# Value stage of an expert-retrieval block: a fixed order for VectorE's work on the operands of a key

## The chip, the cores and the metric

One core of one Trainium2 chip runs the whole program, a single launch. The metric is device time in microseconds of that core. Engines: PE is TensorE (matrix products, with weight loads listed apart as PEld), DVE is VectorE, ACT is ScalarE, POOL is GpSimd, SP is SyncE; SPq is the queue of transfers that SP issues. In this kernel SP issues nearly all plain loads and POOL the gathers.

## What is computed

Two layers of a diffusion backbone on 640 tokens (512 latent, 128 context), width 1024. Each layer is a mixer of three branches and then a product-key expert retrieval. Only the second half of the retrieval is touched here:

```python
u = jnp.take(u_tab, e, axis=0)
act = jax.nn.gelu(jnp.einsum("cd,chkd->chk", hc, u).astype(jnp.float32))
vv = jnp.take(v_tab, e, axis=0)
return jnp.einsum("chk,chkd->cd", (gate * act).astype(hc.dtype), vv)
```

There are 16384 experts, 128 chosen by each token. The table of values `v_tab` has 16384 rows of 1024 floats in each layer.

## The kernel before

The 640 tokens are five tiles of 128. For the tiles in the dense part the kernel doesn't gather: it multiplies all 16384 rows with the tokens and sets what was not chosen to zero by a gate matrix. The first dense stage (`dense_u`, L1675) makes the activations of three tiles and stores them to DRAM as `ad`. The second (`dense_v`, L1693) is the **value stage**: it runs over 128 keys, and a key is a block of 128 rows of the value table.

For each key `operands` (L1705) makes what the products need:

- `vr`, the 128 rows of the table (512 KB, loaded at L1708 through SP, three buffers).
- `gt`, the gates of four keys at once (1024 KB, L1713 through SP, two buffers). Four keys that share one `gt` are called a **group** below.
- `gl`, the gated activations, three buffers. ACT copies one tile's part from `gt` (L1719); SP loads the other three tiles' activations into the rest (192 KB, L1721), and DVE multiplies them with the gates (L1722: *gating*).
- `ash` and `asl`, the high and low half of `gl`: ACT casts (L1725), DVE subtracts (L1726). Three buffers each.
- `us`, the high and low halves of the two 512-column halves of `vr`, made by the helper `split` (L415 on ACT, L416 on DVE). Four buffers of each kind, so two keys' worth.

`products` (L1730) then issues 24 matmuls of 128x512 for a key: four token tiles, two column halves, and for each of these high by high, high by low and low by high (L1737). They add up in eight PSUM banks over all keys.

Beside this, the weave of L1636 puts the *sparse passes* of the remaining tile or tiles into the program: POOL gathers one row for each of 128 tokens (L1529, 512 KB, four buffers) and DVE multiplies or adds it (L1793 `pscr`, L1809 `acc`).

Dependences hold a value back until its buffer is free: `gl` of key n+3 may be written only when L1726 of key n has read the old one, `vr` of key n+3 when both L416 of key n are done, `us` of key n+2 when the products of key n are done. `gt` of a group may be loaded when the last gating and copy of the group two before it are done.

The order of instructions on each engine is not that of the code: a scheduler makes it when the program is built, from its own estimates. Each engine then takes its instructions strictly in that order. `keep_in_program_order` pins only the sparse passes among themselves.

Of the kernel before, what the change touches and what calls it, by code (L numbers as in the profile page):

```python
# [20 lines left out]
D = 1024  # L21
# [25 lines left out]
USB = 4  # L47
# [201 lines left out]
NOSYNC = mybir.DependencyInfo(mybir.DependencyClass.NoSync, mybir.DependencyReason.DATA)  # L249
# [11 lines left out]
class K:  # L261
# [1431 lines left out]
    def dense_v(self, l, gr, ar, grow, x, xr, pool, kp, nxt, sps):  # L1693

        nc, I = self.nc, self.I
        v = nc.vector
        ns, S = NT - ND, ND - NU
        acc = {}  # L1700
        vt = I["pev"]
        gts = {}
        dp = pool

        def operands(n, lo, hi, pool):  # L1705
            w, CT = 128 * (hi - lo), 128 // GC
            vr = dp.tile([128, D], F32, tag="raw", name=self.nm("vr"), bufs=RAWB)
            nc.sync.dma_start(vr, bass.AP(tensor=vt.tensor, offset=vt.offset + (16384 * l + n) * D, ap=[[128 * D, 128], [1, D]]))  # L1708
            if (n // GN, lo, hi) not in gts:
                gts.clear()  # L1710
                t = dp.tile([128, ND * CT, GN, GC], F32, tag="gt", name=self.nm("gt"))
                n0 = n // GN * GN
                nc.sync.dma_start(t[:, CT * lo:CT * hi], gr[CT * lo:CT * hi, :, n0:n0 + GN, :].rearrange("c p n t -> p c n t"))  # L1713
                gts[n // GN, lo, hi] = t
            g = gts[n // GN, lo, hi][:, :, n % GN, :]
            gl = dp.tile([128, 128 * ND], F32, tag="gl", name=self.nm("gl"), bufs=3)
            g3 = gl.rearrange("p (c t) -> p c t", t=GC)
            if lo < S:
                nc.scalar.copy(g3[:, CT * lo:CT * S], g[:, CT * lo:CT * S])  # L1719
            if hi > S:  # L1720
                nc.sync.dma_start(gl[:, 128 * S:], ar[n])  # L1721
                v.tensor_tensor(g3[:, CT * S:], g3[:, CT * S:], g[:, CT * S:], op=ALU.mult)  # L1722
            a = slice(128 * lo, 128 * hi)
            ah, al = (pool.tile([128, 128 * ND], F32R, tag=t, name=self.nm(t), bufs=3 if pool is dp else None) for t in ("ash", "asl"))
            nc.scalar.copy(ah[:, a], gl[:, a])  # L1725
            v.tensor_tensor(al[:, a], gl[:, a], ah[:, a].bitcast(F32), op=ALU.subtract)  # L1726
            vs = [self.split(pool, vr[:, o:o + 512], [128, 512], "us", USB if pool is dp else None) for o in range(0, D, 512)]
            return ah, al, vs

        def products(n, i, hf, ops):  # L1730
            ah, al, vs = ops
            vh, vl = vs[hf]
            if i not in acc:
                acc[i] = [self.psum(t) for t in ACCT[i]]
            c = slice(128 * i, 128 * i + 128)
            for q, (a, b) in enumerate(((ah, vh), (ah, vl), (al, vh))):
                nc.tensor.matmul(acc[i][hf], a[:, c], b, start=n == first(i) and q == 0, stop=n == 127 and q == 2)  # L1737

        def key(n, lo, hi):
            ops = operands(n, lo, hi, dp)  # L1740
            for hf in range(2):
                for i in range(lo, hi):
                    products(n, i, hf, ops)

        m = 0

        def first(i):
            return 0 if i >= S else m

        def done(i):  # L1750
            for hf in range(2):
                d = slice(512 * hf, 512 * hf + 512)
                t = pool.tile([128, 512], F32, tag="gl", name=self.nm("dr"), bufs=3)
                v.tensor_tensor(t, acc[i][hf], grow[1 if ns + i < 4 else 0][:, d], op=ALU.mult)
                self.x_add(ns + i, 512 * hf, t)

        while not self.gated or m % GN:
            key(m, S, ND)
            m += 1
            yield 1.3 * NU  # L1760
        follow = self.x_open(l, x, xr, kp, nxt)
        step = max(1, (128 - m) // max(m, 1))
        late = iter(range(m))
        for n in range(m, 128 - GE):
            key(n, 0, ND)
            yield 1.3 * ND
            if (n - m) % (GN * step) == GN * step - 1 or n == 127 - GN:
                for j in islice(late, None if n == 127 - GN else GN):
                    key(j, 0, S)
                    yield 1.3 * S  # L1770
        zp = xr.enter_context(self.pool("pz", "right", GE - 1))
        tail = [(n, operands(n, 0, ND, zp if n < 127 else dp)) for n in range(128 - GE, 128)]
        run(sps)
        for i in range(ND + 2):
            if i < ND:
                for n, ops in tail:
                    for hf in range(2):
                        products(n, i, hf, ops)
            if i > 0:
                next(follow)  # L1780
            if i < ND:
                done(i)
        self.hT = ret(follow)
# [66 lines left out]
def run(g):  # L1850
    for _ in g:
        pass


def ret(g):
    while True:
        try:
            next(g)
        except StopIteration as e:
            return e.value  # L1860
# [47 lines left out]
```

## Time and profile before

| | us |
|---|---|
| median of 3 runs | 6227.96 |
| lowest and highest of them | 6202.13, 6228.57 |
| the profiled execution's own time | 6218.67 |
| its span, first to last instruction | 6216.6 |

| engine | busy us | share of the span |
|---|---|---|
| PE | 5582.4 | 90% |
| PEld | 4880.7 | 79% |
| DVE | 4162.3 | 67% |
| ACT | 2626.0 | 42% |
| POOL | 1706.5 | 27% |

The mean granted clock of TensorE is 0.934 of full speed. The value stage's products run from 2287 us to 3133 us in layer 0 and from 5390 us to 6201 us in layer 1, a good quarter of the span. Busy shares are means over stages with different limits, so the stage has to be read by itself.

### The profile page before, as it was taken

What the parts mean: (1) busy time and instruction counts of PE and PEld (TensorE: products, weight loads), DVE (VectorE), ACT (ScalarE), POOL (GpSimd) and SP (SyncE); (2) the same over time, 40 slices, a digit from 0 to 9 for tenths busy, and PEclk for the clock granted to TensorE, in tenths of its full rate; (3) what the DMA queues carried; (4) which work ended last, traced back from release to release, by engine and by line L of the source; (5) the groups of instructions that cost most, each with busy time, mean ns of one, the idle gap of its engine ahead of it and who ended that gap; (6) DMA issues with size and microseconds to landing.
All of it is one profiled execution on the core that took longest, in us unless ns stands there. A gap on an engine that the chain in (4) does not pass through costs nothing. (4 is left out here: it accounts for less than half of the span.)

```text
span 6216.6 us, 93203 instructions
## 1 busy us (share of the span) xinstructions
PE 5582.4 (90%) x32966; PEld 4880.7 (79%) x32966; DVE 4162.3 (67%) x9449; ACT 2626.0 (42%) x6243; POOL 1706.5 (27%) x1604
## 2 busy tenths in 40 slices
PE   7899899899799988988988998999987999888988
PEld 5787778789799987767766887788887999777776
DVE  6545545369988876666765545453799888666667
ACT  6244344433366652322352443443333666422223
POOL 1212222101533333333222222231024333233331
PEclk9899899999899999999998888999999999999999
DMA  6212222532589998888852122224325999988886
GB/s 235 73 54 72 69 78 67 181 122 71 156 300 350 341 340 278 296 278 294 270 189 72 48 71 73 76 69 158 103 92 162 340 344 343 325 292 294 283 302 228
DMA packets 630596, 1210.49 MB, mean 195 GB/s; under 512 B 127728, under 2 KB 352368, under 8 KB 630128
## 3 DMA queue, kind: packets, MB, share of 16 engines
q1 hardware_dynamic: 413840, 574.87, 28.1%
q0 software_dynamic: 132768, 469.70, 22.7%
q10 hardware_dynamic: 83520, 159.97, 6.8%
q8 instruction: 259, 4.24, 0.3%
q14 instruction: 209, 1.71, 0.1%
HBM read 1020.28 MB, written 184.05 MB: 194 GB/s over the span
## 5 line engine op out<-in xcount | busy, mean ns | idle before, releaser
L440 PE MATMUL mm<-hT,us 128*128 128x384 f32 x6144 | 1184.4, 348 | 131.4 <-ACT gl L1689 58.6
L440 PEld LDWEIGHTS mm<-hT,us 128*128 128x128 f32 x6144 | 1096.2, 195 | 156.7 <-ACT gl L1689 61.8
L469 PE MATMUL mm<-hT,ws 128*128 128x320 f32 x5472 | 1041.6, 336 | 10.7 <-POOL ws L416 6.7
L1529 POOL DMA_INDIRECT ga<-in_peu,ei x512 | 606.2, 1184 | 1249.9 <-DVE pscr L1793 1139.7
L469 PEld LDWEIGHTS mm<-hT,ws 128*128 128x128 f32 x5472 | 876.0, 202 | 72.3 <-issue 19.6
L1793 DVE SCALAR_TENSOR_TENSOR pscr<-ga,ht 128x1024 bf16<-128x1024 f32 x512 | 627.4, 1225 | 31.5 <-DMA ga<-in_peu,ei 28.8
L416 POOL TENSOR_TENSOR ws<-wr,ws 128x512 fp32r<-128x512 f32 x228 | 302.6, 1329 | 1053.9 <-ACT ws L415 1042.2
L1737 PE MATMUL g<-us,ash 128*128 128x512 f32 x1024 | 349.5, 410 | 192.7 <-DVE us L416 166.5
L1529 POOL DMA_INDIRECT ga<-in_pev,ei x256 | 339.1, 1325 | 630.8 <-DVE acc L1809 570.2
L1719 ACT COPY gl<-gt 128x128 f32<-128x128 f32 x256 | 76.3, 299 | 1010.7 <-DVE asl L1726 984.9
L1722 DVE TENSOR_TENSOR gl<-gl,gt 128x384 f32<-128x384 f32 x256 | 142.2, 556 | 519.5 <-DMA gl<-ad 498.5
L415 ACT CAST ws<-wr 128x512 fp32r<-128x512 f32 x340 | 210.3, 620 | 477.1 <-PE mm L469 186.0
L1737 PEld LDWEIGHTS g<-us,ash 128*128 128x128 f32 x1024 | 199.0, 195 | 268.0 <-DVE us L416 200.2
L416 POOL TENSOR_TENSOR us<-ur,us 128x512 fp32r<-128x512 f32 x132 | 202.6, 1557 | 752.3 <-ACT us L415 566.5
L1659 DVE TENSOR_TENSOR oh<-cst,gm 128x512 f32<-128x512 f32 x512 | 333.2, 684 | 111.4 <-PE g L1663 86.8
L415 ACT CAST us<-ur 128x512 fp32r<-128x512 f32 x512 | 307.1, 616 | 237.8 <-PE mm L440 221.6
L416 DVE TENSOR_TENSOR us<-vr,us 128x512 fp32r<-128x512 f32 x528 | 361.1, 687 | 14.5 <-ACT us L415 14.4
L1662 ACT ACTIVATE oh<-oh,gm 128x128 f32<-128x128 f32 x1024 | 338.3, 394 | 24.2 <-DVE oh L1659 20.3
L415 ACT CAST us<-vr 128x512 fp32r<-128x512 f32 x528 | 324.2, 617 | 32.6 <-PE mm L1737 23.7
L1737 PE MATMUL a<-us,ash 128*128 128x512 f32 x1024 | 331.2, 404 | 4.2 <-ACT ash L1725 4.2
L1737 PE MATMUL c<-us,ash 128*128 128x512 f32 x1024 | 333.1, 406 | 0.0
L1737 PE MATMUL mm<-us,ash 128*128 128x512 f32 x1024 | 327.8, 401 | 0.0
(381 smaller groups left out, 10908.2 us busy)
## 6 DMA issues: line engine op xcount, KB each, us to landing
vr<-in_pev SPq DMA_DIRECT2D x264, 512.0 KB
ur<-in_put SPq DMA_DIRECT2D x256, 512.0 KB
gd<-gmo ACTq DMA_DIRECT2D x128, 512.0 KB
gt<-gd SPq DMA_DIRECT2D x62, 1024.0 KB
wr<-in_win POOLq DMA_DIRECT2D x114, 512.0 KB
aw<-in_adaw SPq DMA_DIRECT2D x96, 512.0 KB
ad<-gl ACTq DMA_DIRECT2D x256, 192.0 KB
gl<-ad SPq DMA_DIRECT2D x256, 192.0 KB
```

What stands on the lines that cost most here:

```text
L415: nc.scalar.copy(h, src)
L416: (eng or nc.vector).tensor_tensor(lo, src, h.bitcast(F32), op=ALU.subtract)
L440: self.nc.tensor.matmul(out, a, b, start=i == 0, stop=i == len(ops) - 1)
L469: self.nc.tensor.matmul(ps, w[k][i], hT[j][:, k, a:b], start=k == i == j == 0, stop=k == 7 and i == 1)
L1529: self.nc.gpsimd.indirect_dma_start(out=t, out_offset=None, in_=self.I[tab], in_offset=bass.IndirectOffsetOnAxis(ap=ei[:, s:s + 1], axis=0))
L1659: v.tensor_tensor(oh[k], iota, T[k][:, t0:t0 + 4, None].to_broadcast([128, 4, 128]), op=ALU.is_equal)
L1662: nc.scalar.mul(oh[0][:, j, :], oh[0][:, j, :], T[2][:, t0 + j:t0 + j + 1])
L1719: nc.scalar.copy(g3[:, CT * lo:CT * S], g[:, CT * lo:CT * S])
L1722: v.tensor_tensor(g3[:, CT * S:], g3[:, CT * S:], g[:, CT * S:], op=ALU.mult)
L1737: nc.tensor.matmul(acc[i][hf], a[:, c], b, start=n == first(i) and q == 0, stop=n == 127 and q == 2)
L1793: pin(v.scalar_tensor_tensor(scr, u, 1.0, h, op0=ALU.mult, op1=ALU.mult, accum_out=dots[:, s:s + 1]))
```

## The change

In `operands` the splits of the two halves of `vr` move from the end to the place right behind the load of `vr`. And all DVE instructions that `operands` makes are chained, each to the one made before it, over all keys, by a dependence that only fixes the order and makes nobody wait on a semaphore. So DVE's order for a key is: low half of the first 512 columns, low half of the second, gating, low half of the activations; then the same for the next key. Sparse passes may still stand anywhere between. No instruction is added or removed, no size or buffer count changes.

```diff
@@ dense_v
         acc = {}
+        self.lastv = None
         vt = I["pev"]
@@ operands
             nc.sync.dma_start(vr, bass.AP(tensor=vt.tensor, offset=vt.offset + (16384 * l + n) * D, ap=[[128 * D, 128], [1, D]]))
+            made = nc.cur_bb.bb.instructions
+            at = len(made)
+            vs = [self.split(pool, vr[:, o:o + 512], [128, 512], "us", USB if pool is dp else None) for o in range(0, D, 512)]
             if (n // GN, lo, hi) not in gts:
...
             v.tensor_tensor(al[:, a], gl[:, a], ah[:, a].bitcast(F32), op=ALU.subtract)
-            vs = [self.split(pool, vr[:, o:o + 512], [128, 512], "us", USB if pool is dp else None) for o in range(0, D, 512)]
+            for i in made[at:]:
+                if i.engine == mybir.EngineType.DVE:
+                    if self.lastv is not None:
+                        self.tc.add_manual_dep(i, self.lastv.name, NOSYNC, reason="hold_order")
+                    self.lastv = i
             return ah, al, vs
```

Line numbers of the changed kernel: L1709 loads `vr`, L1717 `gt`, L1725 `gl`; L1723 is the copy, L1726 the gating, L1729 and L1730 the halves of the activations, L1745 the products, L1801 and L1817 the sparse passes.

What this makes of the order, around key 36 of layer 0 (keys counted from 0 in the order of the program; the number behind a name tells buffers' uses apart). **DVE, before**: `vr_24273` and `us_24286`, `us_24290` belong to key 36, `us_24240` to key 35, `asl_24282` to key 36, `asl_24330` to key 37, `gl_24373` to key 38, `gl_24418` to key 39.

```order
L1722 TENSOR_TENSOR gl_24373<-gl_24373,gt_24275 128x384
L1726 TENSOR_TENSOR asl_24282<-gl_24277,ash_24281 128x512
L416 TENSOR_TENSOR us_24240<-vr_24225,us_24239 128x512
L1793 SCALAR_TENSOR_TENSOR pscr_20803,do_20802<-ga_24267,ht_14562 128x1024
L1793 SCALAR_TENSOR_TENSOR pscr_20803,do_20802<-ga_24270,ht_14562 128x1024
L416 TENSOR_TENSOR us_24286<-vr_24273,us_24285 128x512
L1722 TENSOR_TENSOR gl_24418<-gl_24418,gt_24275 128x384
L1726 TENSOR_TENSOR asl_24330<-gl_24325,ash_24329 128x512
L416 TENSOR_TENSOR us_24290<-vr_24273,us_24289 128x512
```

**DVE, changed**: here `us_24276`, `us_24280`, `gl_24285` and `asl_24290` are all of key 36, and `us_24326` opens key 37.

```order
L1801 SCALAR_TENSOR_TENSOR pscr_20803,do_20802<-ga_24267,ht_14562 128x1024
L416 TENSOR_TENSOR us_24276<-vr_24273,us_24275 128x512
L1801 SCALAR_TENSOR_TENSOR pscr_20803,do_20802<-ga_24270,ht_14562 128x1024
L416 TENSOR_TENSOR us_24280<-vr_24273,us_24279 128x512
L1726 TENSOR_TENSOR gl_24285<-gl_24285,gt_24283 128x384
L1730 TENSOR_TENSOR asl_24290<-gl_24285,ash_24289 128x512
L1801 SCALAR_TENSOR_TENSOR pscr_20803,do_20802<-ga_24317,ht_14562 128x1024
L416 TENSOR_TENSOR us_24326<-vr_24323,us_24325 128x512
```

Before, the gating stood three keys ahead of the splits it stands between; now it stands behind those of its own key. The number of sparse passes for a key (two, two, one) is as it was.

**SP, before** (loads for keys 34 to 39; `vr_24180`, `vr_24225`, `vr_24273` and `vr_24323` are keys 34 to 37, `gl_24277`, `gl_24325`, `gl_24373` and `gl_24418` keys 36 to 39, `gt_24466` the gates of keys 40 to 43):

```order
L1708 DMA vr_24180<-in_pev 128x1024
L1713 DMA gt_24466<-gd_14612 128x16x128
L1708 DMA vr_24225<-in_pev 128x1024
L1721 DMA gl_24277<-ad_14613 128x384
L1721 DMA gl_24325<-ad_14613 128x384
L1708 DMA vr_24273<-in_pev 128x1024
L1721 DMA gl_24373<-ad_14613 128x384
L1708 DMA vr_24323<-in_pev 128x1024
L1721 DMA gl_24418<-ad_14613 128x384
```

**SP, changed** (`vr_24180` to `vr_24323` are keys 34 to 37 again, `gl_24190`, `gl_24235`, `gl_24285` keys 34 to 36, `gt_24283` the gates of keys 36 to 39):

```order
L1709 DMA vr_24180<-in_pev 128x1024
L1717 DMA gt_24283<-gd_14612 128x16x128
L1725 DMA gl_24190<-ad_14613 128x384
L1709 DMA vr_24225<-in_pev 128x1024
L1725 DMA gl_24235<-ad_14613 128x384
L1709 DMA vr_24273<-in_pev 128x1024
L1725 DMA gl_24285<-ad_14613 128x384
L1709 DMA vr_24323<-in_pev 128x1024
```

The activations' load of a key now follows the load of its own rows instead of running two keys ahead, and beside the load of key 34's rows stands the block of keys 36 to 39 where before it was the block of keys 40 to 43.

**ACT, before** (casts at L415 of keys 34 and 35, copies of keys 38 and 39, casts at L1725 of keys 35 and 36):

```order
L415 CAST us_24190<-vr_24180 128x512
L1725 CAST ash_24231<-gl_24227 128x512
L415 CAST us_24194<-vr_24180 128x512
L1719 COPY gl_24373<-gt_24275 128x128
L415 CAST us_24235<-vr_24225 128x512
L1725 CAST ash_24281<-gl_24277 128x512
L415 CAST us_24239<-vr_24225 128x512
L1719 COPY gl_24418<-gt_24275 128x128
```

**ACT, changed** (casts at L415 and at L1729 of keys 34 and 35, copies of keys 36 and 37):

```order
L415 CAST us_24182<-vr_24180 128x512
L1723 COPY gl_24285<-gt_24283 128x128
L415 CAST us_24186<-vr_24180 128x512
L1729 CAST ash_24194<-gl_24190 128x512
L415 CAST us_24227<-vr_24225 128x512
L1723 COPY gl_24333<-gt_24283 128x128
L415 CAST us_24231<-vr_24225 128x512
L1729 CAST ash_24239<-gl_24235 128x512
```

The copy from the gates stands two keys ahead of the casts around it, where it was four, and the cast of the activations is that of the same key as the casts of its rows. PE's order through the middle of the stage and POOL's order are as they were.

## Rows read from the trace of the kernel before

**Rows 1.** Windows: stretch, us; PE, PEld, DVE, ACT, POOL busy; PE's clock, DMA share, GB/s.

```profile
1900.00:2200.00 300.00, 286.71 (x1799) 281.54 (x1797) 249.19 (x418) 198.79 (x499) 102.99 (x89) 0.99 0.95 344
2334.76:3082.68 747.92, 664.02 (x2744) 534.24 (x2743) 505.18 (x726) 217.78 (x457) 253.85 (x194) 0.95 0.84 286
5408.20:6150.07 741.87, 658.46 (x2744) 529.73 (x2743) 506.08 (x726) 217.03 (x457) 254.47 (x194) 0.96 0.85 289
...
2484.70:2506.70 22.00, 22.00 (x99) 18.22 (x98) 17.49 (x31) 7.66 (x16) 7.84 (x7) 1.00 0.93 316
```

**Rows 2.** DMA issues of layer 0's value stage: count and KB each.

```profile
gt<-gd SPq DMA_DIRECT2D x31, 1024.0 KB
```

**Rows 3.** Waits, stretch 2334.76 to 3082.68: us in total, times, longest us.

```profile
DVE gl L1722 <- DMA gl<-ad: 239.8, 66, 11.3
...
PE g L1737 <- DVE us L416: 83.4, 29, 6.7
...
SPq L1721 <- DVE asl L1726: 407.0, 71, 12.5
```

**Rows 4.** Waits of PE in the same stretch of layer 1, 5408.20 to 6150.07.

```profile
PE g L1737 <- DVE us L416: 83.0, 30, 6.7
```

**Rows 5.** Timeline, DVE: start us, us, instruction [idle before <- what ended it].

```profile
2722.26 0.68 DVE L1726 TENSOR_TENSOR asl<-gl,ash 128x512 fp32r<-128x512 f32 x1
...
2723.47 1.28 DVE L1809 SCALAR_TENSOR_TENSOR acc<-ga,do,acc 128x1024 f32<-128x1024 f32 x1
2732.57 0.56 DVE L1722 TENSOR_TENSOR gl<-gl,gt 128x384 f32<-128x384 f32 x1 [7.83 <-DMA gl<-ad]
...
2734.24 0.68 DVE L416 TENSOR_TENSOR us<-vr,us 128x512 fp32r<-128x512 f32 x1
```

**Rows 6.** Timeline, SP's queue of transfers, the same place.

```profile
2719.42 0.37 SPq L1713 DMA_DIRECT2D gt<-gd  x1
2720.57 3.85 SPq L1708 DMA_DIRECT2D vr<-in_pev  x1
2724.48 1.07 SPq L1721 DMA_DIRECT2D gl<-ad  x2
```

**Rows 7.** Timeline, PE: the same group's wait, and products behind the one before.

```profile
2707.82 1.05 PE L1737 MATMUL a<-us,ash 128*128 128x512 f32 x2
...
2709.10 1.05 PE L1737 MATMUL c<-us,ash 128*128 128x512 f32 x2
...
2711.93 0.61 PE L1737 MATMUL a<-us,ash 128*128 128x512 f32 x2
...
2712.61 0.61 PE L1737 MATMUL c<-us,ash 128*128 128x512 f32 x2
...
2734.98 0.80 PE L1737 MATMUL g<-us,ash 128*128 128x512 f32 x1 [4.31 <-DVE us L416]
```

**Rows 8.** DMA busy in tenths, 40 slices of 2719 to 2747 us.

```profile
DMA  9899999999999999974200003789997888698999
```

**Rows 9.** Groups by form, 2334.76 to 3082.68: busy us, mean ns | idle before.

```profile
L1809 DVE SCALAR_TENSOR_TENSOR acc<-ga,do,acc 128x1024 f32<-128x1024 f32 x127 | 162.5, 1280 | 2.0 <-DMA ga<-in_pev,ei 0.5
...
L416 DVE TENSOR_TENSOR us<-vr,us 128x512 fp32r<-128x512 f32 x227 | 156.0, 687 | 0.0
...
L415 ACT CAST us<-vr 128x512 fp32r<-128x512 f32 x227 | 140.0, 617 | 1.6 <-PE mm L1737 1.4
...
L1793 DVE SCALAR_TENSOR_TENSOR pscr<-ga,ht 128x1024 bf16<-128x1024 f32 x69 | 84.1, 1219 | 0.7
L1726 DVE TENSOR_TENSOR asl<-gl,ash 128x512 fp32r<-128x512 f32 x114 | 78.0, 685 | 0.0
...
L1722 DVE TENSOR_TENSOR gl<-gl,gt 128x384 f32<-128x384 f32 x116 | 64.3, 555 | 240.0 <-DMA gl<-ad 239.8
...
L1719 ACT COPY gl<-gt 128x128 f32<-128x128 f32 x114 | 34.1, 299 | 489.6 <-DVE asl L1726 485.9 <-DVE gl L1722 3.7
```

**Rows 10.** Timeline, DVE near the stage's start: activations' low half right behind gating.

```profile
2328.28 0.69 DVE L1726 TENSOR_TENSOR asl<-gl,ash 128x512 fp32r<-128x512 f32 x1 [0.69 <-ACT ash L1725]
```

## The prediction

> **What bounds the kernel now.** I read the windows first. In the middle of layer 0's value stage, 2334.76 to 3082.68 us, PE is busy for 664.02 of 747.92 us and DVE for 505.18; layer 1's stretch is alike [rows 1]. Neither engine is full, and the DMA engines are busy 0.84 and 0.85 of the time. Both ends of a stretch are issues of a block of gates; 31 blocks are loaded in the stage [rows 2] and the stretch runs from the second to the last, so it holds 29 groups of four keys: 25.79 us for a group in layer 0, 25.58 in layer 1. One group (2484.70 to 2506.70) passed without a wait of PE: 22.0 us, PE busy throughout, clock 1.00 [rows 1]. That is the price of a group when PE alone sets the pace.
>
> Who takes the other 3.7 us is in the waits: PE stood 83.4 us in 29 waits for DVE's low half of the rows, while DVE stood 239.8 us in 66 waits for the load of the activations [rows 3]; in layer 1 PE lost 83.0 us in 30 waits [rows 4]. [...]
>
> The timeline of one group shows why DVE is late. At 2732.57 a gating starts after 7.83 us of waiting for its load; the low half that PE needs stands behind it in DVE's order and starts at 2734.24 [rows 5], and PE, idle for 4.31 us, resumes at 2734.98 [rows 7]. The load came late since SP issued it late: at 2719.42 the block, then rows that kept SP for 3.85 us, and only at 2724.48 two loads of activations [rows 6]. They land by 2732.57, at most 8.1 us later. Meanwhile the DMA engines, full for half the group, run empty (the zeros of [rows 8]): no buffer is free, so nothing is issued. It is a ring: activations' low half frees `gl`, SP waits for that (407.0 us in 71 waits [rows 3]), the load flies, the gating waits, and behind the gating stands the next low half. DMA time is not scarce on average; it is asked for in bursts.
>
> **The change, part by part.** Nothing is added or removed, so the sum is one of waits.
>
> *DVE's order.* Before, between the low half of key 36's activations, which frees a buffer, and the gating of key 39, which needs the load into it, DVE has two splits and two passes: 2 x 0.69 + 2 x 1.22 = 3.8 us [rows 9] against a flight of up to 8.1 us. Changed, the gating of the key that gets the buffer comes three keys later: 3 x 5.5 us less one gating, its wait for ACT and the low half (0.56 + 0.69 + 0.69 [rows 9, 10]) = 14.6 us. The cover is nearly four times as long. The longest wait of before, 11.3 us [rows 3], on top of 3.8 makes 15.1, so hardly a wait should be left. I cost the activations' load at nothing; its cover is these three keys.
>
> [...]
>
> *DVE's new idle time.* Gating and low half of the same key now follow each other, and ACT's cast lies between: 0.69 us of idle where the trace has that pair [rows 10]. A key then costs DVE 2 x 0.69 + 0.56 + 0.69 + 0.69, and 196 passes over 116 keys (127 of 1.28 and 69 of 1.22 [rows 9]) add 1.69 x 1.26 = 2.13: 5.45 us, 21.8 a group. Durations in that view overlap a little, so this is an upper end; it is just below PE's 22.0. Keys with two passes take 5.8, keys with one 4.5; `us` buffers for two keys level that. So DVE covers its own idle time, but with little to spare. If it didn't, each 0.1 us more a key would cost 0.4 a group.
>
> *SP and ACT.* SP issues rows and activations of a key side by side, so the pair of activations behind a block goes. But a block's lead shrinks: its buffer comes free with the gating of key 31, and ACT's first copy from it (key 36) stands beside the casts of key 34, where before gating ran three keys and the copy four keys ahead. From the gating of key 31, which frees the buffer, to the cast behind the copy for key 36 PE does over two keys; the flight is at most 13.15 us (2719.42 to 2732.57, when later loads of the same queue had landed [rows 5, 6]). Around this ring: flight, copy 0.30, cast 0.62, split 0.69, gating 0.56, idle 0.69, low half 0.69, passes 2.13, two splits 1.38, gating 0.56 = flight + 7.6. At 13.15 that is 20.8 a group, below 22.0: cost zero as long as the flight stays below 14.4.
>
> *DMA as the next to be late.* The same bytes must fly in less time. Layer 0's 29 groups hold 0.84 x 747.92 = 628 us of DMA time, layer 1's 0.85 x 741.87 = 631. No row shows this stage with full engines for long. Upper end of the rate: the engines full, 628 us, and then PE's 638 (29 x 22.0) decides. The nearest row is the activation stage, 1900 to 2200 us, with gathers and row loads of the same kinds: share 0.95 over 300 us, PE busy for 286.71 [rows 1]. I take 0.95: 628 / 0.95 = 661 and 631 / 0.95 = 664 us, 22.8 a group. Gain 748 - 661 = 87 and 742 - 664 = 78.
>
> *Sum.* 87 + 78 = 165 us. Start (four half-size keys, waits for the gate matrix) and tail of the stage I cost at zero: there DVE has no ring to close. Against the profiled execution's 6218.67: **6054 us**. That execution lies 9 us below the median of the runs shown, which is small beside the range.
>
> **Rivals.**
>
> *PE sets the pace.* DMA engines take the denser stream without delay: 29 x 22.0 = 638 in both layers, gain 110 + 104 = 214: 6005 us. For it: the wait-free group ran with a share of 0.93 [rows 1]. Against it: there part of the loads had come earlier, in the slack that goes away. [...]
>
> *The block of gates becomes the wait, in part.* With fuller engines its flight grows to, say, 17 us; the ring gives 24.6 a group and the gain is 29 x (1.19 + 0.98) = 63: 6156 us. For it: the copy now comes some three keys' time behind the issue, before about four. Against it: 13.15 is itself an upper bound.
>
> *The same ring, slower than before.* It decides from the flight at which flight + 7.6 exceeds 25.7 + 0.54, that is 18.7 us; at 20 us a group takes 27.6, and the loss is 29 x (1.81 + 2.02) = 111: 6330 us. For it: the copy stands in ACT's queue ahead of casts that PE needs. Against it: nothing in this stage has flown that long.
>
> *No change.* The loads stay late because DMA itself is late, and the wait moves with the order: 6219 us. For it: the shares of 0.84 and 0.85. Against it: the empty slices of [rows 8]. That the order isn't what the change says is excluded by the rows of DVE's order.
>
> **How the numbers follow.** Forecast (6025 to 6095) 0.53; PE sets the pace (5985 to 6025) 0.17; the block in part (6095 to 6188) 0.15; no change 0.07; slower 0.08. A measurement of this kernel can tell about 0.5%, 31 us, from no change. Faster by more than that: 0.53 + 0.17 + 0.15 = 0.85; within it 0.07; slower 0.08. The range takes forecast, the PE case and most of the third, 5985 to 6155, and leaves out 0.04 of that and the 0.15 of the last two: 0.19.
>
> **What would show it.** In the profile after: groups of 22 to 23.6 us between issues of blocks; DVE's waits for the activations' load below 40 us a layer instead of 240; PE's waits for DVE below 25; clock 0.98; DMA share near 0.95; 0.6 to 0.7 us of DVE idle in front of each low half of the activations. It would be wrong if ACT's copy waited for the block, if DVE waited for gathers, or if groups stayed above 25 us.

## The result, and the profile after

| | before | after |
|---|---|---|
| median of 4 runs each, us | 6228.26 | 5976.58 |
| lowest and highest | 6202.13, 6236.26 | 5955.84, 5989.45 |
| the profiled execution's own time | 6218.67 | 5986.22 |
| its span | 6216.6 | 5984.2 |

The ratio of after to before is 0.960, 95% interval 0.9567 to 0.9633: faster by 3.7 to 4.3%. The forecast was 6054 with a range down to 5985; the median lies 8 us below that range. The sign and the mechanism came as forecast, the size did not: 165 us were forecast, 232.4 us went from the profiled span.

The windows of the changed kernel, to be laid beside [rows 1] (same columns; the first two stretches are again bounded by issues of a block of gates, 30 of them in either kernel in layer 0; the third is 19 of the intervals between them, undisturbed ones):

```profile
2342.87:2971.64 628.77, 628.09 (x2770) 519.67 (x2770) 513.74 (x745) 241.04 (x467) 223.74 (x192) 1.00 0.97 342
5293.27:5920.24 626.97, 626.97 (x2768) 519.13 (x2767) 514.41 (x744) 240.23 (x464) 227.09 (x192) 1.00 0.97 344
2471.16:2884.61 413.45, 413.45 (x1826) 342.35 (x1825) 338.89 (x464) 157.90 (x305) 154.43 (x132) 1.00 0.99 348
```

PE is busy almost without a gap (628.09 of 628.77 us) at a granted clock of 1.00. A group takes 413.45 / 19 = 21.76 us. The stretches shrank by 747.92 - 628.77 = 119.2 and 741.87 - 626.97 = 114.9 us, together 234.1: the change of the span, 232.4, comes from here. That the two agree within 2 us is partly luck: the rest of the program, which the change doesn't touch, took 4683 to 4743 us in the profiles of this document. (The four runs of the change differ alike, and with the mean clock: 0.945, 0.944, 0.940 and 0.937 at spans of 5953.7, 5964.9, 5984.2 and 5987.4 us.) So nothing was given back elsewhere beyond this scatter, and small effects have to be read from the stretches and not from total times.

The waits of layer 0's stretch, 2340 to 2960 us, beside [rows 3], which cover the longer stretch of before (748 us):

```profile
ACT us L415 <- PE mm L1745: 198.9, 192, 1.9
...
DVE asl L1730 <- ACT ash L1729: 77.6, 113, 0.7
DVE us L416 <- ACT us L415: 37.0, 32, 3.6
ACT gl L1723 <- DMA gt<-gd: 17.0, 10, 5.7
...
PE g L1745 <- ACT ash L1729: 1.4, 1, 1.4
```

DVE's 239.8 us for the load of the activations are gone from the list, and so are PE's 83.4 us for DVE. The longest wait among those that make `us` is now ACT's for PE: it waits until products have freed a buffer of `us`, so the operands run ahead of PE instead of behind it. Over the whole program the gating's own line (busy, mean ns, idle before) reads

```profile
L1726 DVE TENSOR_TENSOR gl<-gl,gt 128x384 f32<-128x384 f32 x256 | 141.2, 552 | 2.4 <-DMA gl<-ad 2.2 <-issue 0.2
```

so 2.2 us of waiting for loads in both layers together. One group's DVE timeline, beside [rows 5], shows the new order and its price, the 0.69 us in front of each low half of the activations:

```profile
2605.99 0.69 DVE L416 TENSOR_TENSOR us<-vr,us 128x512 fp32r<-128x512 f32 x1
2606.59 0.55 DVE L1726 TENSOR_TENSOR gl<-gl,gt 128x384 f32<-128x384 f32 x1
2607.83 0.69 DVE L1730 TENSOR_TENSOR asl<-gl,ash 128x512 fp32r<-128x512 f32 x1 [0.69 <-ACT ash L1729]
2608.44 1.28 DVE L1817 SCALAR_TENSOR_TENSOR acc<-ga,do,acc 128x1024 f32<-128x1024 f32 x1
...
2617.71 0.69 DVE L416 TENSOR_TENSOR us<-vr,us 128x512 fp32r<-128x512 f32 x1 [1.95 <-ACT us L415]
```

The last row has another cause. DVE stood 1.95 us for ACT's cast, and ACT was late because its copy out of `gt` had waited for the block of gates:

```profile
2616.86 0.30 ACT L1723 COPY gl<-gt 128x128 f32<-128x128 f32 x1 [2.76 <-DMA gt<-gd]
2617.06 0.61 ACT L415 CAST us<-vr 128x512 fp32r<-128x512 f32 x1
```

ACT's copy waited for a block 10 times in this stretch, 17.0 us together, which the prediction had named as a sign of being wrong. It cost PE nothing, since the operands are ahead: PE's waits for ACT or DVE sum to 1.4 us.

### The profile page after: what moved, and what is told of

It reads as the page before. It is cut to its first block, busy times and chain, and to the rows that moved or that the text cites. A ratio compares the mean times of both kernels' runs of the same rounds, so it can differ in the third digit from the quotient of the medians.

```text
span 5984.2 us, 92691 instructions
## 1 busy us (share of the span) xinstructions
PE 5516.9 (92%) x32966; PEld 4858.7 (81%) x32966; DVE 4163.3 (70%) x9449; ACT 2664.8 (45%) x6243; POOL 1656.7 (28%) x1604
## 5 line engine op out<-in xcount | busy, mean ns | idle before, releaser
L1529 POOL DMA_INDIRECT ga<-in_peu,ei x512 | 592.4, 1157 | 1168.9 <-DVE pscr L1801 1059.7
L1801 DVE SCALAR_TENSOR_TENSOR pscr<-ga,ht 128x1024 bf16<-128x1024 f32 x512 | 628.1, 1227 | 37.1 <-DMA ga<-in_peu,ei 35.7
L415 ACT CAST us<-vr 128x512 fp32r<-128x512 f32 x528 | 327.6, 622 | 450.3 <-PE mm L1745 440.9
L1529 POOL DMA_INDIRECT ga<-in_pev,ei x256 | 300.4, 1173 | 501.2 <-DVE acc L1817 465.0
L415 ACT CAST ws<-wr 128x512 fp32r<-128x512 f32 x340 | 210.3, 620 | 489.2 <-PE mm L469 203.8
L415 ACT CAST us<-ur 128x512 fp32r<-128x512 f32 x512 | 306.8, 616 | 237.5 <-PE mm L440 216.7
L1745 PE MATMUL a<-us,ash 128*128 128x512 f32 x1024 | 319.8, 394 | 23.0 <-ACT ash L1729 23.0
L1745 PE MATMUL g<-us,ash 128*128 128x512 f32 x1024 | 319.1, 393 | 15.4 <-ACT ash L1729 15.4
L1817 DVE SCALAR_TENSOR_TENSOR acc<-ga,do,acc 128x1024 f32<-128x1024 f32 x254 | 324.9, 1279 | 0.4 <-DMA ga<-in_pev,ei 0.4
L1745 PE MATMUL c<-us,ash 128*128 128x512 f32 x1024 | 318.6, 392 | 0.0
L1730 DVE TENSOR_TENSOR asl<-gl,ash 128x512 fp32r<-128x512 f32 (+2 forms) x264 | 178.6, 677 | 201.0 <-ACT ash L1729 199.7
L1745 PE MATMUL mm<-us,ash 128*128 128x512 f32 x1024 | 317.9, 392 | 0.0
L1729 ACT CAST ash<-gl 128x512 fp32r<-128x512 f32 (+2 forms) x264 | 160.2, 608 | 353.2 <-DVE gl L1726 340.6
```

Source lines behind the costliest of these rows:

```text
L415: nc.scalar.copy(h, src)
L1529: self.nc.gpsimd.indirect_dma_start(out=t, out_offset=None, in_=self.I[tab], in_offset=bass.IndirectOffsetOnAxis(ap=ei[:, s:s + 1], axis=0))
L1801: pin(v.scalar_tensor_tensor(scr, u, 1.0, h, op0=ALU.mult, op1=ALU.mult, accum_out=dots[:, s:s + 1]))
L1817: pin(v.scalar_tensor_tensor(acc, u, w[:, s:s + 1], acc, op0=ALU.mult, op1=ALU.add))
```

## The experiments

Ratios are to the kernel before, measured again beside each run, with their 95% intervals; the change itself stands at 0.9567 to 0.9633. The last column is the length of both layers' stretches in the run's profile, between the same issues of blocks as above: 1489.8 us before, 1255.7 in the change.

| run | what | median us | interval of the ratio | stretches, us |
|---|---|---|---|---|
| e1 | splits moved in the code, no chain | 6216.41 | 0.998 to 1.0041 | 1484.1 |
| e2 | chain over the old code's order | 5961.74 | 0.953 to 0.964 | 1262.2 |
| e3 | before, with four buffers of `gl` | 6199.99 | 0.9946 to 0.9996 | 1472.1 |
| e5 | the change, with two buffers of `gl` | 6112.25 | 0.9792 to 0.9893 | 1416.5 |
| e7 | chain, gating one key ahead, three buffers | 6043.32 | 0.9661 to 0.9762 | 1335.7 |
| e8 | the same, four buffers | 6032.48 | 0.9659 to 0.9748 | 1318.7 |
| e10 | e8 with ACT's order fixed too | 6092.91 | 0.9788 to 0.9828 | 1383.9 |
| e4 | the change, 128 KB a key more, issued elsewhere | 5972.46 | 0.9555 to 0.9656 | 1256.2 |
| e4 | the same, 208 KB | 5988.23 | 0.9572 to 0.9689 | 1255.7 |
| e9 | the change, 128 KB a key more to load | 5975.24 | 0.9583 to 0.9659 | 1256.1 |
| e9 | the change, 208 KB a key more to load | 5975.53 | 0.9585 to 0.9658 | 1274.6 |
| e6 | the change, 16 products a key | 5949.44 | 0.955 to 0.9609 | 1263.4 |

The tag `gl` is used in the activation stage and at the end of a layer too, so e3, e5, e8 and e10 change the number of buffers there as well; this is another reason to read them by the stretches.

### Which part of the change does it

**e1: the move alone.**

```diff
+            vs = [self.split(...) for o in range(0, D, 512)]
             if (n // GN, lo, hi) not in gts:
...
-            vs = [self.split(...) for o in range(0, D, 512)]
```

> Only the place of the splits in the code, no chain. DVE's order comes out as before: a gating still stands three keys ahead of the split behind it. Ring theory (the distance on DVE between the low half that frees an activations' buffer and the gating that needs the load into it decides): no gain, 6228 us within 25; DVE waits for the activations' load about 240 us a layer, PE for DVE about 83. Rival (making the low halves of the rows early in the code is what helps): near the changed kernel, 5977 us.

Measured: no difference from before. Its waits, same stretch:

```profile
DVE gl L1723 <- DMA gl<-ad: 194.5, 55, 8.6
...
PE g L1737 <- DVE us L416: 63.0, 24, 6.4
```

The scheduler ordered DVE as before, so moving the lines in the code did nothing; both waits of [rows 3] stand.

**e2: the chain alone,** over the old code's order (gating, low half of the activations, then both splits), shown as an edit of the kernel before.

```diff
+            made = nc.cur_bb.bb.instructions
+            at = len(made)
...
             vs = [self.split(...) for o in range(0, D, 512)]
+            for i in made[at:]:
+                if i.engine == mybir.EngineType.DVE:
...
```

> Only the chain, in the old order of the code: gating, low half of the activations, then the two low halves of the rows of a key. The distance from freeing a buffer to the next gating in it is three keys as in the changed kernel. Ring theory: 5965 to 6010 us, DVE waits for the activations' load below 20 us a layer. Rival (the rows' low halves have to come first, as in the change): PE's waits for DVE's low half of the rows stay, 6080 to 6230 us.

Measured 5961.74 us; its interval overlaps that of the change. Its window has PE busy all the time:

```profile
2340.00:2960.00 620.00, 620.00 (x2736) 513.25 (x2735) 507.89 (x739) 235.66 (x461) 232.90 (x192) 1.00 0.97 345
```

So it is the chain that acts; that the splits stand first in a key is not what the time comes from. (The chain names DVE's instructions alone, but the scheduler's order on SP and ACT changed with it; which part of the gain needs that, no run separates.) In both orders gating and activations' low half of one key are neighbours, and the next gating into that buffer comes three keys later.

### The cover: from the low half that frees a buffer to the gating that needs its load

**e3: one more buffer instead of an order.**

```diff
-            gl = dp.tile([128, 128 * ND], F32, tag="gl", name=self.nm("gl"), bufs=3)
+            gl = dp.tile([128, 128 * ND], F32, tag="gl", name=self.nm("gl"), bufs=4)
```

> The kernel before with four buffers of activations instead of three; DVE's order is as before. The cover of the load grows by one key, from 3.8 to about 9.3 us, against a flight of up to 8.1 us. Ring theory: most of the gain without any chain, 5980 to 6080 us, DVE's waits for that load below 80 us a layer instead of 240. Rival (the order itself matters, by the bursts on SP and ACT): 6180 us or more.

A miss: 6199.99 us, barely below before.

```profile
DVE gl L1722 <- DMA gl<-ad: 196.8, 55, 9.5
...
PE g L1737 <- DVE us L416: 74.0, 24, 6.8
```

DVE's order shows why: the scheduler let gating run one key further ahead. Between the low half that frees a buffer and the gating that takes it, now four keys later instead of three, stand again mostly two or three splits and one to three passes. Counted over keys 20 to 119 in the traces, DVE's work in between has a median of 3.93 us in both kernels, and so the waits stayed. A buffer is worth nothing if the order spends it.

**e5: one buffer fewer under the new order.** The cover falls by one key of 5.5 us, from 14.6 to about 9.0.

```diff
-            gl = dp.tile([128, 128 * ND], F32, tag="gl", name=self.nm("gl"), bufs=3)
+            gl = dp.tile([128, 128 * ND], F32, tag="gl", name=self.nm("gl"), bufs=2)
```

> The changed kernel with two buffers of activations instead of three; DVE's order is as in the change. The cover of the load falls from 14.6 to about 9 us. Ring theory with a flight of at most 8.1 us also in the denser stream: 5975 to 6030 us. If the flight has grown with the full DMA engines (to 11 us or more), each key waits 2 us: 6100 us or more.

6112.25: the first case missed, the second came, so a load does take longer than 8.1 us. It did so before the change too: e1, with the order and the waits of before, has landings of the activations' loads up to 12.4 us after their issue. The waits, and the loads' count, KB and median us from issue to landing between 2471 and 2850 us:

```profile
DVE gl L1726 <- DMA gl<-ad: 94.4, 25, 6.8
...
PE g L1745 <- ACT ash L1729: 44.1, 19, 4.3
```

```profile
gt<-gd SPq DMA_DIRECT2D x15, 1024.0 KB, 12.6
gl<-ad SPq DMA_DIRECT2D x61, 192.0 KB, 5.9
```

25 waits in some 25 groups: one load in four is late. SP's queue shows which, the one that is issued behind the block of gates and is itself 5.17 us on the queue; between 2360 and 2940 us all 23 waits are for such a load:

```profile
2575.28 0.37 SPq L1717 DMA_DIRECT2D gt<-gd  x1
2576.65 5.17 SPq L1725 DMA_DIRECT2D gl<-ad  x1
```

Its buffer came free, and it was issued, at 2576.6; the gating two keys later is the one that waits, on DVE:

```profile
2590.17 0.56 DVE L1726 TENSOR_TENSOR gl<-gl,gt 128x384 f32<-128x384 f32 x1 [2.97 <-DMA gl<-ad]
```

That is 2590.17 - 2576.65 = 13.5 us from issue to use; the longest landing in this trace is 15.1. Cover plus longest wait estimates the time that the worst load needs from the freeing of its buffer: 9.0 + 6.8 = 15.8 us here, 3.8 + 11.3 = 15.1 before. With 14.6 of cover the change comes close enough that hardly a wait is left.

**e7: another fixed order,** in which gating is that of the next key and stands in front of the key's own low half. Three buffers; by the same count the cover is 9.6 us.

```diff
+            gl = ready.pop(n) if n in ready and (lo, hi) == (0, ND) else gated(n, lo, hi)
+            if (lo, hi) == (0, ND) and n + 1 < 128 - GE and n != 127 - GN:
+                ready[n + 1] = gated(n + 1, lo, hi)
```

> The changed kernel, still chained, but DVE's order for a key is: two low halves of its rows, gating of the NEXT key, low half of its own activations. A buffer of activations is then held one key longer: with three buffers the cover of the load is two keys less gating and low half, 2 x 5.44 - 1.25 = 9.6 us, nearly that of the run with two buffers (9.0 us, 6112 us). Cover theory: 6060 to 6120 us, DVE waits for the activations' load 60 to 100 us a layer. Rival (any fixed order does it): 5960 to 5990 us.

Measured 6043.32, a little better than expected and clearly behind the change. "Any fixed order does it" is therefore wrong.

```profile
DVE gl L1724 <- DMA gl<-ad: 82.4, 26, 6.2
...
PE g L1754 <- DVE asl L1739: 23.0, 14, 2.9
```

The sum holds again: 9.6 + 6.2 = 15.8. Matched key by key in the traces, the covers are as estimated: from the end of the low half that frees the buffer to the point at which DVE was ready for the gating it is in the median 3.8 us before, 8.8 in e5, 9.5 here and 14.4 in the change, and the longest time from freeing to a gating that had to wait is 16.0, 15.1 and 15.5 us in the first three.

**e8: the same with four buffers.**

```diff
-GLB = 3
+GLB = 4
```

> The same order with four buffers of activations: cover 3 x 5.44 - 1.25 = 15.1 us. Cover theory: 5955 to 5990 us, hardly a wait for the load, groups of 21.8 us. Rival (gating has to stand behind the low halves of its own key): as with three buffers, 6060 us or more.

A miss: 6032.48 is hardly better than e7. The wait for the activations' load left the list, as it should with a key more of cover, and others took its place:

```profile
DVE us L417 <- ACT us L416: 138.8, 74, 8.6
...
ACT gl L1721 <- DMA gt<-gd: 102.1, 23, 8.8
...
PE g L1754 <- DVE asl L1739: 18.5, 13, 2.6
```

With a buffer more, ACT's copy out of `gt` can run further ahead, reaches the block before it has landed, and stops; behind it in ACT's order stand the casts that DVE needs. This is the "block of gates" rival of the prediction, in another kernel than the one it was forecast for. In the change the same wait is 17.0 us in this stretch, and PE doesn't feel it. That this chain of waits is what e8 lost its time to is read from the waits; e10, meant to test it, took them away and brought others.

**e10: ACT's order fixed as well,** to keep the copy from running ahead.

```diff
+                elif i.engine == mybir.EngineType.Activation:
+                    if self.lasta is not None:
+                        self.tc.add_manual_dep(i, self.lasta.name, NOSYNC, reason="hold_order")
+                    self.lasta = i
```

> The run with gating a key ahead and four buffers, and now ACT's instructions of a key are chained too, in the order of the code: two casts of the rows, copy from the gates for the next key, cast of the activations. The first copy from a block then stands three keys later on ACT. If the run before lost its 55 us to ACT's copy waiting for the block of gates (102 us of such waits in 620): 5955 to 5990 us and those waits below 20 us. If something else: 6020 us or more.

A miss, and worse: 6092.91. The wait for the block went, the wait for the activations' load came back, in spite of four buffers:

```profile
DVE gl L1724 <- DMA gl<-ad: 118.1, 29, 7.4
...
PE g L1758 <- DVE asl L1739: 44.8, 18, 4.1
```

SP's queue shows what moved. In e8 the activations' load of a key is issued in front of the block:

```profile
2616.14 0.33 SPq L1729 DMA_DIRECT2D vr<-in_pev  x1
2617.21 0.32 SPq L1723 DMA_DIRECT2D gl<-ad  x1
2617.58 0.43 SPq L1715 DMA_DIRECT2D gt<-gd  x1
```

In e10 it is issued behind it, and is 4.53 us on the queue:

```profile
2614.28 0.33 SPq L1729 DMA_DIRECT2D vr<-in_pev  x1
2614.79 0.37 SPq L1715 DMA_DIRECT2D gt<-gd  x1
2615.21 4.53 SPq L1723 DMA_DIRECT2D gl<-ad  x1
```

But the place behind the block is not enough to explain it. In the change, too, that load is issued behind the block, and it was longer on the queue than here; its gating, three keys after the one that freed the buffer, started without a wait:

```profile
2601.73 0.37 SPq L1717 DMA_DIRECT2D gt<-gd  x1
2602.39 0.69 DVE L1730 TENSOR_TENSOR asl<-gl,ash 128x512 fp32r<-128x512 f32 x1 [0.69 <-ACT ash L1729]
2603.11 6.86 SPq L1725 DMA_DIRECT2D gl<-ad  x1
2618.32 0.55 DVE L1726 TENSOR_TENSOR gl<-gl,gt 128x384 f32<-128x384 f32 x1
```

There the load left at 2603.11, as soon as the low half had freed its buffer (2602.39 + 0.69). In e10 the buffer of the load at 2615.21 was free at 2610.11 + 0.69 = 2610.80, so 4.4 us went by before the issue, and the gating waited:

```profile
2610.11 0.69 DVE L1739 TENSOR_TENSOR asl<-gl,ash 128x512 fp32r<-128x512 f32 x1
2627.42 0.56 DVE L1724 TENSOR_TENSOR gl<-gl,gt 128x384 f32<-128x384 f32 x1 [2.28 <-DMA gl<-ad]
```

It stood on SP behind the load of the rows, which had to wait for DVE to free its own buffer. SP's waits in e10, 2340 to 2960 us, begin with

```profile
SPq L1729 <- DVE us L417: 334.4, 67, 11.2
```

and have none of the activations' load (L1723) for the low half that frees its buffer. From the freeing to the issue it takes 4.8 us in e10 in the median and 0.0 in the change, in e5, e7 and e8. So four buffers gave 15.7 us of cover, and the order on SP used up a third of it. DVE's distance is not the whole cover: what counts is the part of it behind the load's issue, and fixing one engine's order moved that.

### Is DMA the limit at 0.95?

**e4: extra loads that nobody reads,** 128 and 208 KB a key from the value table, written beside the load of `gl`. For the first, about 6050 us were expected at a limit and 5975 to 5995 with room; for the second:

> The same with 208 KB for each full key, 0.85 MB more a group, 8.3 MB. At a limit of 348 GB/s: 23.9 us a group, about 6100 us. With room up to 382 GB/s: 5975 to 5995 us.

The times, ratios 0.9605 (128 KB) and 0.9631 (208 KB), say nothing of a limit: no such load is issued within the stretches, and 349 and 348 GB/s moved between 2471 and 2850 us, as in the change. The scheduler had put them ahead of the stage. So these two runs are the change in the stretch, and their traces have what the change's own lacks, times of landing. For the activations' loads with 208 KB, 2360 to 2940 us:

```profile
DMA to landing us min/median/max: 3.8/9.2/14.4
```

The slowest of them just fits the change's cover, 14.4 us in the median.

**e9: the same loads, each held behind the key's load of `gl` on SP** (256 columns are 128 KB, 416 are 208 KB).

```diff
+                    ex = dp.tile([128, 256], F32, tag="ex", name=self.nm("ex"), bufs=2)
+                    nc.sync.dma_start(ex, ...)
+                    two = [i for i in made[at:] if i.engine == mybir.EngineType.SP][-2:]
+                    self.tc.add_manual_dep(two[1], two[0].name, NOSYNC, reason="hold_order")
```

> The changed kernel with one more load of 128 KB for each full key, this time held in place in SP's order behind the load of the key's activations: 8.0 MB a group instead of 7.5. If 348 GB/s is the DMA engines' limit: 23.0 us a group, about 6050 us. If they have room to 367 GB/s: 21.8 us a group, 5970 to 5995 us.

> The same with 208 KB for each full key: 8.3 MB a group. At a limit of 348 GB/s: 23.9 us a group, about 6100 us. With room to 382 GB/s: 5970 to 5995 us.

Both take the time of the change in total. In the stretches only the first does (1256.1 us); the second takes 1274.6, 19 us more, hidden in its total since the rest of that execution was shorter. The window 2471 to 2850 us, with 128 KB and then with 208 KB a key:

```profile
2471.00:2850.00 379.00, 379.00 (x1674) 313.83 (x1673) 310.69 (x426) 145.34 (x280) 141.74 (x122) 1.00 1.04 374
```

```profile
2471.00:2850.00 379.00, 375.60 (x1642) 306.76 (x1642) 304.11 (x416) 137.04 (x273) 144.33 (x119) 1.00 1.05 381
```

With 374 GB/s PE still never waits. At 381 it loses 3.4 of 379 us, groups take 22.1 in the mean, and ACT begins to wait for loads:

```profile
ACT gl L1723 <- DMA gt<-gd: 73.8, 27, 5.5
ACT us L415 <- DMA vr<-in_pev: 56.5, 40, 3.1
```

In the change these are 17.0 and 3.0 us. With these loads in this order the room thus ends between 374 and 381 GB/s, 348 are used, and a busy share of 0.95 was never a limit. Whether the rate itself ends it or the longer way through SP's order isn't separated.

### What comes behind PE

**e6: eight matmuls fewer a key.**

```diff
-            for q, (a, b) in enumerate(((ah, vh), (ah, vl), (al, vh))):
+            for q, (a, b) in enumerate(((ah, vh), (ah, vl))):
```

> The changed kernel without the product of the activations' low half with the rows' high half: 16 matmuls a key instead of 24, so PE needs 14.5 us a group. What is next shows as the length of a group: 20.3 to 21.0 us if DVE is next, 21.5 us if the DMA engines are at 348 GB/s, below 19 us if neither. In time: 5900 to 5970 us in the first two cases, 5820 us or less in the third.

5949.44 us: a third of PE's work in the stage gone, and hardly any time with it; the stretches are no shorter at all, 1263.4 us against 1255.7. The window, and two low halves of consecutive keys on DVE:

```profile
2471.00:2850.00 379.00, 279.65 (x1116) 207.92 (x1115) 307.54 (x429) 147.16 (x280) 155.64 (x121) 0.98 0.98 348
```

```profile
2605.74 0.69 DVE L1730 TENSOR_TENSOR asl<-gl,ash 128x512 fp32r<-128x512 f32 x1 [0.69 <-ACT ash L1729]
...
2611.18 0.69 DVE L1730 TENSOR_TENSOR asl<-gl,ash 128x512 fp32r<-128x512 f32 x1 [0.68 <-ACT ash L1729]
```

Here DVE runs without a gap but for the 0.69 us: 5.44 us for this key with two passes, and undisturbed groups of 19.8 to 20.2 us. But the mean group is still 21.9, since loads interrupt (ACT waits 63.2 us for rows in the stretch). Why they do so at 348 GB/s, when 374 flew in e9 without a wait of PE, these runs don't settle. What they show is that less work on PE alone gains nothing here, and that PE (21.76) and DVE (about 20) lie close together: the next gain has to move both, and the loads' waits with them.

## Why the prediction was right or wrong

- **What bound the kernel: right.** That it is the ring of buffer, issue, flight and gating, and not the sum of any engine's work, is shown from both sides: the same order with another place in the code changes nothing (e1), the chain alone gives all of the gain but 6.5 of 234 us (e2), and less cover under the same chain brings the waits back (e5, e7). That a late load holds back what stands behind its gating is in the trace of before: the low half that starts at 2734.24 [rows 5] had its cast from ACT by 2725.96 (2725.34 + 0.62, the last cast ahead of it), and PE had used up its products by 2730.67 (2734.98 - 4.31 [rows 7]), so nothing that it reads or writes was missing for 3.5 us or more; it stood behind the gating that had waited 7.83 us for its load.
- **DVE's order: right in its result, one of its two numbers wrong.** DVE's waits for loads were forecast below 40 us a layer and are 2.2 in two layers. But of the two numbers for what the cover has to hold, the flight of "at most 8.1 us" was too small: it was read from the issue of two loads that SP sent together, while e1 has landings up to 12.4 us in the old order and e5 shows loads that stick behind the block. The other, "makes 15.1", was right, and e5 and e7 give 15.8. The cover is indeed nearly four times the old one, but it is only just enough.
- **DVE's new idle time: right.** 77.6 / 113 = 0.69 us a key. The 21.8 us a group were indeed an upper end: e6 measured about 20. DVE has 1.8 us a group to spare, more than forecast.
- **The block's ring: right as to its cost, not its number.** "Cost zero as long as the flight stays below 14.4" rested on a flight of at most 13.15. The trace of the change has no landing times; in e2, equally fast, blocks took 9.2 to 15.1 us, median 12.2, and in e4 with 208 KB 8.6 to 15.3, and PE lost nothing. Single flights above the threshold did no harm there, presumably since a group's slack carries over to the next. The rival "block of gates" came in the change as 17.0 us of ACT's waits without a price, and in e8 in earnest.
- **DMA: wrong, and this is the step that failed.** "I take 0.95: 628 / 0.95 = 661 and 631 / 0.95 = 664 us, 22.8 a group." It treats the busy share as fixed work. It isn't: the same bytes (286 x 747.92 = 213.9 MB, 342 x 628.77 = 215.0 MB) took 628 us of busy share before and 0.97 x 628.77 = 610 after. And 0.95 is not a ceiling: e9 shows 1.04 with PE never waiting. The row taken as nearest, the activation stage at 0.95, is one where PE was busy for 286.71 of 300 us and its waits were for DVE and ACT (5.9 and 7.3 us) and none for a load, so it showed what that stage asked for and not what the engines can give. Without this term the sum is the rival "PE sets the pace": 214 us and 6005, which had 0.17. The row that spoke for it was at hand, the group without waits at 0.93.
- **The last 20 us: a small size.** 29 x 22.0 = 638 came from one group; the stretches measured 628.77 and 626.97, 9 and 11 us less. The 22.00 us lie between two issues on SP, not between two groups on PE, and hold 99 matmul records where a group has 96. [Rows 7] had the better price: three matmuls in 0.68 us make 32 x 0.68 = 21.76 for a group, which is what the change measures. That is 29 x 0.24 = 7 us a layer. The rest is in the ends of the stretch: it runs from the third full block, not the second, and its 30 issues include the 256 KB block of the keys left for later, so it holds 2770 matmul records in the change and not 29 x 96 = 2784. 165 for the sum, 49 for the DMA term and 20 for this give 234, what the stretches lost.
- **Clock and outside of the stretch: right.** The clock rose from 0.95 to 1.00 (0.98 forecast). Before, behind a gap, three matmuls took 1.28 us, soon after 0.68 [rows 7], at granted clocks of 0.58 and 1.00 (windows of the kernel before, below). So the clock takes what PE's waits leave of layer 0's old loss: with 21.76 a group it is 747.92 - 631.0 - 83.4 = 33 us, and 664.02 us busy at a mean clock of 0.95 make the same 631. And start and tail cost nothing beyond the scatter of the rest: 234.1 in the stretches, 232.4 in the span.

```profile
2707.00:2709.10 2.10, 2.08 (x6) 1.62 (x7) 2.10 (x4) 1.02 (x3) 0.79 (x1) 0.58 0.29 33
2711.93:2720.00 8.07, 8.07 (x37) 6.71 (x36) 6.01 (x9) 1.98 (x5) 3.83 (x4) 1.00 0.88 293
```

## What to carry to other kernels

Where a load is late though DMA has room, count on the consumer's engine from the instruction that frees the buffer to the one that needs the next load, take off what the load waits on its issuing queue after its buffer is free, and compare that with the longest wait plus the present distance: that sum (15 to 16 us here) is what an order or a buffer has to cover. An extra buffer without a fixed order can be spent by the scheduler (e3: 3.93 us of DVE's work in between, as before), and a fixed order on one engine moves the loads on another (from the freeing of the buffer to the issue it is 0.0 us in the median in e8 and 4.8 in e10), so the order on every engine of the ring has to be read again. A DMA busy share is no price and 1.0 no ceiling (e9: 1.04 at 374 GB/s, without a wait of PE): to learn how much room there is, put more bytes in place and see when somebody waits, and read it from the stretch, since totals scatter by more than it.

## What the runs showed of the hardware that was not expected

The busy share of the DMA engines, as this profile counts the time of packets, goes above 1: 1.04 at 374 GB/s and 1.05 at 381, each over 379 us. It rose far less than the rate did, from 0.84 at 286 GB/s: the time counted for a byte fell by 6% between 286 and 381 GB/s, 0.84 / 286 = 0.00294 against 1.05 / 381 = 0.00276. Part of this may be the mix, since e9 adds loads of its own; with the same bytes, from before to the change, it is 0.00294 against 0.97 / 342 = 0.00284, 3%.

The rate, too, went above what the rows of before hold: 344 GB/s is the highest of [rows 1], and one core, the only one that the program runs on, moved 381 GB/s over 379 us (e9 with 208 KB). What it can move beyond that, no run shows.
